# A decoder layer's first feed-forward block: ScalarE and VectorE in written order, five more low halves by adding transfers, one down step moved

## The chip, the cores and the metric

One core of a Trainium2 chip runs the whole layer in one launch. The metric is the device time of a run in microseconds. TensorE (PE) multiplies, VectorE (DVE) and ScalarE (ACT) work elementwise, GpSimd (POOL) and SyncE (SP) here mostly issue transfers.

## The reference

A macaron layer on 512 tokens of width 1024: half a SwiGLU, a mixing stage, half a second SwiGLU, each on an RMS-normed input.

```python
for l in range(DEPTH):
    x = x + 0.5 * swiglu(rms_norm(x, g_ffn1[l]), w_ffn1_gate[l], w_ffn1_up[l], w_ffn1_down[l])
    h = rms_norm(x, g_mix[l])
    proj = h @ w_in[l]
    ...                       # windowed attention, causal conv, attention to 256 memory tokens
    x = x + jnp.concatenate([y_attn, y_conv, y_mem], axis=-1) @ w_out[l]
    x = x + 0.5 * swiglu(rms_norm(x, g_ffn2[l]), w_ffn2_gate[l], w_ffn2_up[l], w_ffn2_down[l])

def swiglu(x, w_gate, w_up, w_down):
    return (jax.nn.silu(x @ w_gate) * (x @ w_up)) @ w_down
```

D_FF is 2816, 22 tiles of 128 hidden channels. All is float32. The change touches the two SwiGLU blocks.

## The kernel before

**Splitting.** x is kept transposed: 8 tiles `x[:, k]` of 128 channels by 512 tokens. Each operand of a product is split into a high half in the short format (float32r) and a low half, the rest: w = hi + lo. A product is three matmuls, hi·hi, hi·lo and lo·hi (`mm3`, L363 to L373, for 512 tokens; `product`, L464 to L471, for 256). The high half is a cast on ScalarE (L173, hidden tiles L427), the low half a subtraction on VectorE (L178, L428). For some weights the low half is made another way ("by queue"): ScalarE writes -hi into the low half's buffer (L175), and POOL issues a transfer that reads the weight from HBM once more and adds it there (L176).

**Weights.** `Weights` holds one list of weight tiles in the order of use. `load_to` issues loads on SP into 4 raw buffers, `split_to` makes hi and lo in 4 split buffers, in list order; `next()` hands out a weight and first splits `conv_ahead` (3) further ones. `load_piece` and `split_piece` do the first two weights by halves.

**A block.** The first tiles are direct (tiles 0 to 3 in block one, 0 to 2 in block two): gate and up are 24 matmuls of 512 tokens each. While they run, VectorE and ScalarE make the blocks of the normed x (`blocks(k)`, k = 0 to 3: seven sums of quarters, split in hi `bh` and lo `bl`) that the remaining, fast tiles need: those are one step of Strassen's scheme (`fast`, 84 matmuls of 256 tokens, weights g, s12, s43, u; the sums s12 and s43 on VectorE, L128 to L131, the second half of u as `vhi` and `vlo`). `evac` multiplies gate and up by the norm's factor `rb` and applies silu; `hidden` splits the result into `hh` and `hl`. xh, xl, hh and hl share a ring of N_ACT = 20 buffers, taken in turn: 16 by xh and xl, then two pairs of hidden tiles; the third hidden tile takes the buffer of xh 0.

**Down steps.** `Plan` divides the hidden tiles into rounds; after a round, the down product of these tiles is added to x, output tile by output tile, each weight load serving two of them. The first round's four loads come in block one as three before tile 4 and one inside tile 5, in block two as four before tile 3. Results of the first two loads go to x by an adding transfer from POOL (L528), the others by VectorE (L531).

**Order.** A scheduler sets every engine's order from its own cost model; nothing is pinned by hand before the change. Ahead of the first tile, the row sums of x² for the norm are gathered on VectorE (L397), reduced on TensorE (L402), turned into factors by a dozen operations on 4 columns (L404 to L407) and spread by four transposes (L415). The first tile's products run over x tiles in the groups `STARTS`.

```python
STARTS = [(0,), (1,), (2, 3), (4, 5), (6, 7)]
PIECES = {(0,): slice(0, 512), (2, 3): slice(512, 1024)}
W.add(down(*d), OTHER if d[0] else WIDE, n == 2 and d[0] == 0)
W.add(flat(gu[f, i]), WIDE, n == 2 and f > 1)
early = self.loads(0) if self.direct < 4 else self.loads(0)[:-1]
```

Of the kernel before, what the change touches and what calls it, by code (L numbers as in the profile page):

```python
# [30 lines left out]
F32 = mybir.dt.float32  # L31
# [4 lines left out]
ALU = mybir.AluOpType  # L36
# [24 lines left out]
PIECES = {(0,): slice(0, 512), (2, 3): slice(512, 1024)}  # L61
# [23 lines left out]
class Weights:  # L85
# [63 lines left out]
    def split_to(self, n):  # L149
        nc = self.nc  # L150
        while self.done < min(n, len(self.items)):
            i = self.done
            need, cols, off, src = self.items[i]
            self.load_to(need + 1)
            if need in self.after:
                self.after.pop(need)()
            if off is None:
                c = (HALF - 128) // 4
                hi, lo = (
                    self.extra.tile([P, cols + 64], F32R, tag=t, name=f"{t}{i}", bufs=1)[:, c : c + cols] for t in ("vhi", "vlo")  # L160
                )
            else:

                j = self.turn % self.bufs[1]
                c = off // 4
                self.turn += 1
                both = self.pool.tile([P, 2048 + 64], F32R, tag=f"w{j}", name=f"w{i}", bufs=1)
                hi, lo = both[:, c : c + 1024], both[:, c + 1024 : c + 2048]
            if i < self.by_hand:
                self.piece[i] = (src(), hi, lo)  # L170
            else:
                raw = src()
                nc.scalar.copy(hi[:, :cols], raw[:, :cols])  # L173
                if i in self.by_queue:
                    nc.scalar.activation(lo[:, :cols], hi[:, :cols].bitcast(F32), AF.Copy, scale=-1.0)  # L175
                    nc.gpsimd.dma_start(self.shaped(lo, self.loads[need]), self.loads[need], accum_op=ALU.add)  # L176
                else:
                    nc.vector.tensor_tensor(lo[:, :cols], raw[:, :cols], hi[:, :cols].bitcast(F32), op=ALU.subtract)  # L178
            self.split[i] = (hi, lo)
            self.done += 1  # L180
            if i >= self.by_hand:
                self.load_to(need + 1 + self.dma_ahead)

    def load_piece(self, i, c):
        self.nc.sync.dma_start(self.piece[i][0][:, c], self.loads[i][:, c])
# [13 lines left out]
class Plan:  # L199
# [12 lines left out]
    def steps(self, f):  # L212
# [4 lines left out]
        if f < second[1]:  # L217
            early = self.loads(0) if self.direct < 4 else self.loads(0)[:-1]
            late = self.loads(0)[len(early) :]
            return early if f == second[0] else [], late if f == second[0] + 1 else [], []  # L220
# [11 lines left out]
def layer(tc, ctx, a):  # L232
# [35 lines left out]
    def ffn_weights(n, memory):  # L268
# [48 lines left out]

    nc.scalar.dma_start(par, a["par"])
    warm = tmp.tile([P, T], BF16, tag="t", name="warm", bufs=5)
# [7 lines left out]
    W.split_to(2)  # L327
# [57 lines left out]
    class Norm:  # L385
# [5 lines left out]
        def add(self, d, engine=POOL):  # L391
            sq = work() if d else tmp.tile([P, T], F32, tag="sqsum", name=nm("sqsum"), bufs=1)
            ACT.activation(sq, x[:, d], AF.Square)
            if d == 0:
                self.sum = sq
            else:
                (engine if d < KT - 1 else DVE).tensor_tensor(self.sum, self.sum, sq, op=ALU.add)  # L397

# [19 lines left out]
    def ffn(pool, norm, first, gain, hooks, next_gain, last):  # L418
# [120 lines left out]

        held = []  # L540
        nxt = Norm()
        raw = {}
        for f in range(NF):
# [714 lines left out]
```

## Time and profile before

| | |
|---|---|
| median of 3 runs | 862.86 us (862.74 to 863.13) |
| the profiled execution | 863.53 us, its span 861.7 us |
| TensorE busy | 851.7 us, 99% of the span, clock granted 0.999 |
| VectorE busy | 692.9 us, 80% |
| ScalarE busy | 453.6 us, 53% |
| POOL busy | 34.0 us, 4% |
| HBM read | 88.07 MB |

A row of a timeline is: start and length in us, engine, line, operation, out<-in, and in brackets how long the engine stood before it and who ended that. Rows of waits are: who waited for whom, us in total, times, the longest. Rows of transfers end with KB each and the us from issue to landing. Line numbers are those of the kernel before.

### The profile page before, as it was taken

To read this page: it belongs to the slowest core of one execution; us is meant where nothing else is said; L and a number is where in the kernel's file an instruction comes from. 1 tells how busy PE (TensorE), PEld (TensorE's weight loads), DVE (VectorE), ACT (ScalarE), POOL (GpSimd) and SP (SyncE) were. 2 spreads that over 40 slices of the span, in tenths; PEclk is the share of its full clock that TensorE was granted. 3 is DMA by queue.
4 is the path that set the end of the run, shared out by engine and by line. 5 is a ranking of instruction groups with operands and counts; after the bars stand their busy time and mean duration, and the time that the engine had idled before them with its cause. 6 is when DMAs were issued, how large, how long until landed. Compare 5 with 4: busy or idle time off the path is not lost.

```text
span 861.7 us, 15812 instructions
## 1 busy us (share of the span) xinstructions
PE 851.7 (99%) x6421; PEld 791.2 (92%) x6421; DVE 692.9 (80%) x1162; ACT 453.6 (53%) x758; POOL 34.0 (4%) x36
## 2 busy tenths in 40 slices
PE   8999999999999999999999999999999999999998
PEld 5889999999999999988676888889999999999998
DVE  6998977787878897869989985899787878687663
ACT  7465555445554444633948764756554545545440
POOL 0000000000000000300000021210000000000000
PEclk9999999999999999999999999999999999999999
DMA  7435333334453434232010323863433343333312
GB/s 269 127 89 149 106 100 121 100 110 136 119 167 119 123 110 129 74 98 62 13 43 21 118 91 102 187 142 110 122 99 123 99 122 98 110 90 121 92 56 99
DMA packets 36217, 94.07 MB, mean 109 GB/s; under 512 B 3376, under 2 KB 7984, under 8 KB 36144
## 3 DMA queue, kind: packets, MB, share of 16 engines
q1 hardware_dynamic: 32032, 85.99, 32.3%
q0 software_dynamic: 2960, 5.51, 3.9%
q10 hardware_dynamic: 1152, 1.57, 0.6%
q8 instruction: 50, 0.82, 0.4%
q14 instruction: 23, 0.19, 0.1%
HBM read 88.07 MB, written 2.10 MB: 105 GB/s over the span
## 4 chain that ended last, share of the span: by engine, by line
PE 91%; DVE 4%; ACT 2%; DMA 1%; issue 1%; SPq 0%; ACTq 0%; DVEq 0%
PE mm L371 15%; PE mm L373 15%; PE mm L372 15%; PE mm L471 11%; PE mm L469 11%; PE mm L470 11%; PE sc L471 2%; PE sc L470 2%; PE sc L469 2%; PE sc L371 1%; PE sc L372 1%; PE sc L373 1%; PE tp L971 1%; DVE w L178 1%; ACT p L936 1%
## 5 line engine op out<-in xcount | busy, mean ns | idle before, releaser
L469 PE MATMUL mm<-bh,w 128*128 128x256 f32 x888 | 245.5, 276 | 0.8 <-ACT kept L484 0.8
L470 PE MATMUL mm<-bl,w 128*128 128x256 f32 x888 | 245.3, 276 | 0.0
L471 PE MATMUL mm<-bh,w 128*128 128x256 f32 x888 | 245.2, 276 | 0.0
L372 PE MATMUL mm<-hl,w 128*128 128x256 f32 (+1 forms) x648 | 185.0, 286 | 0.0
L373 PE MATMUL mm<-hh,w 128*128 128x256 f32 (+1 forms) x648 | 184.9, 286 | 0.0
L371 PE MATMUL mm<-hh,w 128*128 128x256 f32 (+1 forms) x648 | 184.7, 286 | 0.0
L469 PEld LDWEIGHTS mm<-bh,w 128*128 128x128 f32 x888 | 166.7, 188 | 1.1 <-ACT kept L484 1.0
L470 PEld LDWEIGHTS mm<-bl,w 128*128 128x128 f32 x888 | 166.7, 188 | 0.1
L471 PEld LDWEIGHTS mm<-bh,w 128*128 128x128 f32 x888 | 166.7, 188 | 0.0
L173 ACT CAST w<-wraw 128x1024 fp32r<-128x1024 f32 (+2 forms) x123 | 123.3, 1007 | 76.1 <-PE mm L373 23.7
L178 DVE TENSOR_TENSOR w<-wraw,w 128x1024 fp32r<-128x1024 f32 (+2 forms) x117 | 137.0, 1177 | 27.2 <-ACT w L173 23.5
L371 PEld LDWEIGHTS mm<-hh,w 128*128 128x128 f32 x648 | 121.6, 188 | 2.4 <-ACT hh L427 0.3
L373 PEld LDWEIGHTS mm<-hh,w 128*128 128x128 f32 x648 | 121.7, 188 | 2.2
L372 PEld LDWEIGHTS mm<-hl,w 128*128 128x128 f32 x648 | 121.6, 188 | 2.2
L178 DVE TENSOR_TENSOR w<-s,w 128x1024 fp32r<-128x1024 f32 x74 | 90.4, 1222 | 38.1 <-PE mm L471 32.9
L173 ACT CAST w<-s 128x1024 fp32r<-128x1024 f32 x74 | 77.7, 1052 | 23.5 <-PE mm L471 19.1
L371 PE MATMUL mm<-xh,w 128*128 128x512 f32 x176 | 69.7, 400 | 1.9 <-ACT w L189 1.0
L372 PE MATMUL mm<-xl,w 128*128 128x512 f32 x176 | 69.4, 394 | 0.6 <-DVE xl L383 0.5
L373 PE MATMUL mm<-xh,w 128*128 128x512 f32 x176 | 69.1, 393 | 0.0
L531 DVE SCALAR_TENSOR_TENSOR x<-mm,x 128x512 f32<-128x512 f32 x80 | 54.2, 682 | 7.1 <-PE mm L373 7.1
L490 ACT ACTIVATE t<-t 128x512 f32<-128x512 f32 x37 | 23.4, 633 | 68.7 <-DVE t L489 68.7
L128 DVE TENSOR_TENSOR s<-wraw 128x512 f32<-128x512 f32 x37 | 25.6, 691 | 34.5 <-DMA wraw<-in_wgu 34.4
(247 smaller groups left out, 1378.3 us busy)
## 6 DMA issues: line engine op xcount, KB each, us to landing
wraw<-in_wgu SPq DMA_DIRECT2D x86, 512.0 KB, 3.6
wraw<-in_wd SPq DMA_DIRECT2D x38, 512.0 KB, 3.6
wraw<-in_win SPq DMA_DIRECT2D x12, 512.0 KB, 3.5
wraw<-in_wd SPq DMA_DIRECT2D x8, 384.0 KB, 3.3
x<-t POOLq DMA_DIRECT2D x8, 256.0 KB, 4.1
out<-t SPq DMA_DIRECT2D x7, 256.0 KB, 2.0
x<-in_xT SPq DMA_DIRECT2D x3, 512.0 KB, 7.2
wraw<-in_wout_a SPq DMA_DIRECT2D x6, 256.0 KB, 2.7
```

The source lines that it names most:

```text
L128: nc.vector.tensor_tensor(s12[:, l], u[:, l], u[:, r], op=ALU.add)
L173: nc.scalar.copy(hi[:, :cols], raw[:, :cols])
L178: nc.vector.tensor_tensor(lo[:, :cols], raw[:, :cols], hi[:, :cols].bitcast(F32), op=ALU.subtract)
L371: PE.matmul(ps[:, t], wh[:, w], hi(k)[:, t], start=one, stop=False, skip_group_check=cut > 1)
L372: PE.matmul(ps[:, t], wh[:, w], lo(k)[:, t], start=False, stop=False, skip_group_check=cut > 1)
L373: PE.matmul(ps[:, t], wl[:, w], hi(k)[:, t], start=False, stop=end, skip_group_check=cut > 1)
L469: PE.matmul(ps, wh[:, c], bh[k][:, block], start=one, stop=False, skip_group_check=not first)
L470: PE.matmul(ps, wh[:, c], bl[k][:, block], start=False, stop=False, skip_group_check=not first)
L471: PE.matmul(ps, wl[:, c], bh[k][:, block], start=False, stop=end, skip_group_check=not first)
L490: ACT.activation(g, g, AF.Silu)
L531: DVE.scalar_tensor_tensor(o, ps, 0.5, xd, op0=ALU.mult, op1=ALU.add)
L936: ACT.activation(self.p[n, h][:, c], src[h][:, i, c], AF.Exp, scale=self.fac[:, m : m + 1], bias=self.neg[:, m : m + 1], accum_out=self.de ...
```

## The change

Five things. (1) The beginning (transfers of the first pieces, x, the first weights) and ScalarE's and VectorE's work through x's split, the norm's squares and block one's direct tiles is put under `manual_schedule`: these engines then run in the order in which the code stands. TensorE's order is still the scheduler's. (2) The first two weights come in three pieces of 256, 256 and 512 columns, the first from ScalarE's queue, and x tile by tile is multiplied in the order hi, lo, weight's lo, gate and up in turns. (3) In block one the low halves of tile 3's two weights and of the three early down loads are made by queue. (4) `conv_ahead` is 2 in direct tiles of block one, with explicit `ahead(n)` calls; the first `vhi` (item 14) is split by hand at the end. (5) In block two the first round's last down load moves from before tile 3 into tile 4, and its low half is made by VectorE.

```diff
-PIECES = {(0,): slice(0, 512), (2, 3): slice(512, 1024)}
+PIECES = {0: slice(0, 256), 2: slice(256, 512), 4: slice(512, 1024)}
...
-            early = self.loads(0) if self.direct < 4 else self.loads(0)[:-1]
-            late = self.loads(0)[len(early) :]
+            early, late = self.loads(0)[:-1], self.loads(0)[-1:]
...
-                W.add(down(*d), OTHER if d[0] else WIDE, n == 2 and d[0] == 0)
+                W.add(down(*d), OTHER if d[0] else WIDE, True)
...
-                    W.add(flat(gu[f, i]), WIDE, n == 2 and f > 1)
+                    W.add(flat(gu[f, i]), WIDE, f >= 4 - n)
...
+    W.split_to(2)
+    first = tc.manual_schedule(engines={mybir.EngineType.Activation, mybir.EngineType.SP})
+    first.__enter__()
     nc.scalar.dma_start(par, a["par"])
+    for i in range(2):
+        W.load_piece(i, PIECES[0], nc.scalar)
...
-        if ks in PIECES:
+        c = PIECES.get(ks[-1] + 1)
+        if c:
             for i in range(2):
-                W.load_piece(i, PIECES[ks])
+                W.load_piece(i, c, nc.sync)
     W.load_to(4)
-    nc.scalar.dma_start(ident, a["ident"])
+    nc.sync.dma_start(ident, a["ident"])
+    first.__exit__(None, None, None)
...
+        def ahead(n):
+            if not last:
+                W.split_to(n)
...
+        if not last:
+            order.enter_context(tc.manual_schedule(engines={mybir.EngineType.Activation, mybir.EngineType.DVE}))
...
+            W.conv_ahead = 3 if last or f >= plan.direct else 2
...
+                        for k in ks:
+                            w = slice(k * P, (k + 1) * P)
+                            for i, (one, two) in enumerate(((0, xh), (0, xl), (1, xh))):
+                                for ps, both in ((g, (gh, gl)), (u, (uh, ul))):
+                                    PE.matmul(ps, both[one][:, w], two[k], start=k == i == 0, stop=k == 7 and i == 2)
...
                         raw[0] = evac(0, *held)
-                        blocks(0)
                         hidden(0, raw[0])
+                        ahead(6)
                     uh, ul = W.next()
                     mm3(u, uh, ul, range(8), xhk, xlk, True, True)
+                    ahead(7)
                     raw[f] = evac(f, g, u)
                     hidden(f, raw[f])
+                    if f == 1:
+                        ahead(8)
+                        blocks(0)
+                        ahead(9)
+                    if f == 2:
+                        ahead(11)
                     blocks(f)
-                if f == plan.direct - 1 < 3:
-                    blocks(3)
+                if f == plan.direct - 1:
+                    for k in range(f + 1, 4):
+                        blocks(k)
+                    if not last:
+                        W.split_item(14)
+                    order.close()
...
+    with tc.manual_schedule(engines={mybir.EngineType.Activation, mybir.EngineType.DVE}):
+        for k in range(KT):
             scaled_split(k, C_G1)
-        if ks in PIECES:
-            for i in range(2):
-                W.split_piece(i, PIECES[ks])
-    W.split_to(3)
-    for k in range(KT):
-        norm.add(k, DVE)
+            if k in PIECES:
+                for i in range(2):
+                    W.split_piece(i, PIECES[k])
+            if k in (3, 5):
+                sqs[k // 4] = norm.square(k // 4)
+            if k == 6:
+                take(0)
+                take(1)
+        W.split_to(3)
+        for k in range(2, KT):
+            sqs[k] = norm.square(k)
+            if k > 2:
+                take(k - 1)
+        take(KT - 1)
```

The instructions' order at three places. First ScalarE at the start (xh: high half of an x tile, odd numbers 3, 5, 7, 9 for x tiles 0 to 3; w0, w1: the first two weights; sqsum and t: squares). Before:

```order
L382 ACTIVATE xh_3_119<-x_69,par_67 128x512
L393 ACTIVATE sqsum_19_166<-x_69 128x512
L189 CAST w0_93<-wraw0_92 128x512
L189 CAST w1_95<-wraw1_94 128x512
L382 ACTIVATE xh_5_127<-x_69,par_67 128x512
L393 ACTIVATE t_20_168<-x_69 128x512
L382 ACTIVATE xh_7_131<-x_69,par_67 128x512
L393 ACTIVATE t_21_171<-x_69 128x512
L382 ACTIVATE xh_9_135<-x_69,par_67 128x512
```

And of the change (its own line numbers):

```order
L390 ACTIVATE xh_3_126<-x_69,par_67 128x512
L192 CAST w0_75<-wraw0_74 128x256
L192 CAST w1_77<-wraw1_76 128x256
L390 ACTIVATE xh_5_134<-x_69,par_67 128x512
L390 ACTIVATE xh_7_138<-x_69,par_67 128x512
L192 CAST w0_75<-wraw0_74 128x256
L192 CAST w1_77<-wraw1_76 128x256
L390 ACTIVATE xh_9_146<-x_69,par_67 128x512
L401 ACTIVATE sqsum_11_150<-x_69 128x512
L390 ACTIVATE xh_12_152<-x_69,par_67 128x512
```

The squares moved behind x tile 3 and the weights come in quarters, the second quarter behind x tile 2.

Second, ScalarE in block one around hidden tile 2 (hh_58; w9 and w10 the second and third early down load, bh the high half of a block). Before:

```order
L427 CAST hh_48_374<-kept_47_371 128x512
L456 CAST bh_52_382<-braw_50_378 128x768
L173 CAST w9_476<-wraw9_342 128x1024
L460 CAST bh_52_382<-bmade_51_379 128x1024
L436 ACTIVATE t_56_451<-t_56_451 128x512
L173 CAST vhi14_675<-wraw12_479 128x512
L456 CAST bh_62_465<-braw_60_461 128x768
L427 CAST hh_58_457<-kept_57_454 128x512
```

And of the change:

```order
L450 ACTIVATE t_56_468<-t_56_468 128x512
L441 CAST hh_58_474<-kept_57_471 128x512
L177 CAST w9_478<-wraw9_367 128x1024
L179 ACTIVATE w9_478<-w9_478 128x1024
L177 CAST w10_484<-wraw10_383 128x1024
L179 ACTIVATE w10_484<-w10_484 128x1024
L470 CAST bh_62_494<-braw_60_490 128x768
```

Down load w9 was cast ahead of hidden tile 2 and stands behind it now, with its negated copy.

Third, ScalarE in block two around hidden tiles 0 and 1 (w137: the second early down load). Before:

```order
L427 CAST hh_612_6042<-kept_606_6025 128x512
L456 CAST bh_609_6032<-braw_607_6028 128x768
L436 ACTIVATE t_614_6076<-t_614_6076 128x512
L173 CAST w137_6101<-wraw101_5912 128x768
L175 ACTIVATE w137_6101<-w137_6101 128x768
L460 CAST bh_609_6032<-bmade_608_6029 128x1024
L173 CAST vhi143_6325<-wraw105_6135 128x512
L427 CAST hh_616_6082<-kept_615_6079 128x512
```

And of the change:

```order
L441 CAST hh_607_6048<-kept_606_6045 128x512
L177 CAST vhi142_6317<-wraw104_6125 128x512
L470 CAST bh_615_6096<-braw_613_6092 128x768
L177 CAST w137_6121<-wraw101_5932 128x768
L179 ACTIVATE w137_6121<-w137_6121 128x768
L441 CAST hh_611_6088<-kept_610_6085 128x512
L474 CAST bh_615_6096<-bmade_614_6093 128x1024
```

The cast vhi of tile 3's second weight moved ahead of block 0's high half, and reads load 104 instead of load 105.

More of the change, by code (lines that the diff above doesn't have):

```diff
@@ L149, in split_to @@
     def split_to(self, n):
-        nc = self.nc
[L151 to L161, printed above, removed]
-            else:
[L164 to L182, printed above, removed]
@@ L184, in load_piece, with split_item @@
-    def load_piece(self, i, c):
-        self.nc.sync.dma_start(self.piece[i][0][:, c], self.loads[i][:, c])
+        while self.done < min(n, len(self.items)):
+            if self.done not in self.split:
+                self.split_item(self.done)
+            self.done += 1
+    def split_item(self, i):
+        nc = self.nc
+        need, cols, off, src = self.items[i]
+        self.load_to(need + 1)
+        if need in self.after:
+            self.after.pop(need)()
+        if off is None:
+            c = (HALF - 128) // 4
+            hi, lo = (
+                self.extra.tile([P, cols + 64], F32R, tag=t, name=f"{t}{i}", bufs=1)[:, c : c + cols] for t in ("vhi", "vlo")
+            )
+        else:
+            j = self.turn % self.bufs[1]
+            c = off // 4
+            self.turn += 1
+            both = self.pool.tile([P, 2048 + 64], F32R, tag=f"w{j}", name=f"w{i}", bufs=1)
+            hi, lo = both[:, c : c + 1024], both[:, c + 1024 : c + 2048]
+        if i < self.by_hand:
+            self.piece[i] = (src(), hi, lo)
+        else:
+            raw = src()
+            nc.scalar.copy(hi[:, :cols], raw[:, :cols])
+            if i in self.by_queue:
+                nc.scalar.activation(lo[:, :cols], hi[:, :cols].bitcast(F32), AF.Copy, scale=-1.0)
+                nc.gpsimd.dma_start(self.shaped(lo, self.loads[need]), self.loads[need], accum_op=ALU.add)
+            else:
+                nc.vector.tensor_tensor(lo[:, :cols], raw[:, :cols], hi[:, :cols].bitcast(F32), op=ALU.subtract)
+        self.split[i] = (hi, lo)
+        if i >= self.by_hand:
+            self.load_to(need + 1 + self.dma_ahead)
@@ L187, in split_piece, with load_piece @@
+    def load_piece(self, i, c, queue):
+        queue.dma_start(self.piece[i][0][:, c], self.loads[i][:, c])
     def split_piece(self, i, c):
@@ L389, in __init__, with square, take @@
             self.sum = None
-        def add(self, d, engine=POOL):
+        def square(self, d):
             sq = work() if d else tmp.tile([P, T], F32, tag="sqsum", name=nm("sqsum"), bufs=1)
             ACT.activation(sq, x[:, d], AF.Square)
+            return sq
+        def take(self, d, sq, engine):
             if d == 0:
@@ L397, in add @@
                 (engine if d < KT - 1 else DVE).tensor_tensor(self.sum, self.sum, sq, op=ALU.add)
+        def add(self, d, engine=POOL):
+            self.take(d, self.square(d), engine)
         def stats(self):
@@ L542, in ffn @@
         raw = {}
+        order = ExitStack()
+        if not last:
+            order.enter_context(tc.manual_schedule(engines={mybir.EngineType.Activation, mybir.EngineType.DVE}))
         for f in range(NF):
             pre, mid, post = plan.steps(f)
+            W.conv_ahead = 3 if last or f >= plan.direct else 2
             for d in pre:
@@ L555, in ffn @@
                     for ks in first:
-                        mm3(g, gh, gl, ks, xhk, xlk, ks[0] == 0, ks[-1] == 7)
-                        mm3(u, uh, ul, ks, xhk, xlk, ks[0] == 0, ks[-1] == 7)
+                        if len(ks) > 2:
+                            mm3(g, gh, gl, ks, xhk, xlk, ks[0] == 0, ks[-1] == 7)
+                            mm3(u, uh, ul, ks, xhk, xlk, ks[0] == 0, ks[-1] == 7)
+                            continue
+                        for k in ks:
[3 more added lines that the diff above has]
+                                    PE.matmul(ps, both[one][:, w], two[k], start=k == i == 0, stop=k == 7 and i == 2)
                     norm.stats()
@@ L587, in layer, with take @@
     norm = Norm()
-    for ks in STARTS:
-        for k in ks:
-            scaled_split(k, C_G1)
-        if ks in PIECES:
-            for i in range(2):
-                W.split_piece(i, PIECES[ks])
-    W.split_to(3)
-    for k in range(KT):
-        norm.add(k, DVE)
+    sqs = {}
+    def take(k):
+        norm.take(k, sqs.pop(k), DVE)
+    with tc.manual_schedule(engines={mybir.EngineType.Activation, mybir.EngineType.DVE}):
+        for k in range(KT):
+            scaled_split(k, C_G1)
+            if k in PIECES:
[12 more added lines that the diff above has]
+        take(KT - 1)
     mk = keep.tile([P, 2, ML], F32, name="mk")
```

1 line of the change is left out of this document (removed).

## The prediction

> **What bounds the kernel now.** First the page's head, then who TensorE waits for, then stages.
>
> ```profile
> span 861.7 us, 15812 instructions
> PE 851.7 (99%) x6421; PEld 791.2 (92%) x6421; DVE 692.9 (80%) x1162; ACT 453.6 (53%) x758; POOL 34.0 (4%) x36
> ...
> PE tp L326 <- DVE pair L339: 1.2, 1, 1.2
> PE mm L371 <- ACT w L189: 1.0, 1, 1.0
> ...
> PE mm L371 <- ACT xh L382: 0.9, 1, 0.9
> PE mm L469 <- ACT kept L484: 0.8, 1, 0.8
> PE mm L372 <- DVE xl L383: 0.5, 1, 0.5
> ```
>
> TensorE is busy for 851.7 of 861.7 us, and the change removes no matmul from its list. All that any reordering can move is TensorE's waiting: some 10 us in the whole run. The waits that lie where the change works are the start (L326, L371 on the first weight piece and on xh, L372 on xl) and one single wait of 0.8 us in the second block (L469). Everything else that the change does runs beside a busy TensorE and counts only if it makes TensorE wait.
>
> How full the neighbours are in those stages (columns: length; busy time of PE, PEld, DVE, ACT, POOL; granted clock; DMA share; GB/s):
>
> ```profile
> 32.00:64.00 32.00, 32.00 (x142) 26.30 (x141) 31.75 (x47) 17.93 (x23) 1.89 (x2) 1.00 0.25 73
> 535.00:573.00 38.00, 38.00 (x172) 31.40 (x171) 33.47 (x57) 24.72 (x34) 10.07 (x10) 1.00 0.90 188
> ```
>
> In the first block's direct tiles (32 to 64 us) VectorE has no air, 31.75 of 32, while the DMA share is 0.25; in the second block, which already makes low halves by adding transfers, the DMA share is 0.90. The clock is 1.00 throughout. So moving low halves from VectorE to transfers has room in the first block; the question is whether the transfers come in time.
>
> **Part one, the start.** TensorE's rows before:
>
> ```profile
> 6.12 0.50 PE L371 MATMUL mm<-xh,w 128*128 128x512 f32 x1 [1.01 <-ACT w L189]
> 8.86 0.73 PE L371 MATMUL mm<-xh,w 128*128 128x512 f32 x2 [0.91 <-ACT xh L382]
> ...
> 20.71 0.95 PE L402 MATMUL tp<-ones,sqsum 128*128 128x1 f32 x8
> ...
> 32.13 0.39 PE L371 MATMUL sc<-xh,w 128*128 128x512 f32 x1
> ...
> 43.01 0.39 PE L371 MATMUL mm<-xh,w 128*128 128x512 f32 x1
> ```
>
> From 32.13 to 43.01 stand the 48 matmuls of one direct tile, without a wait: 0.227 us each. Tiles 0 and 1 are 96 matmuls, 21.8 us, but they take 32.13 - 6.12 = 26.0 us. About 1.2 of the difference are the norm's row sums (20.71) and transposes; the other 3.0 are waits. They can go in part. What cannot go is the arrival of x:
>
> ```profile
> x<-in_xT SPq DMA_DIRECT2D x1, 512.0 KB, 6.7
> x<-in_xT SPq DMA_DIRECT2D x1, 512.0 KB, 7.9
> ...
> 9.35 0.72 ACT L382 ACTIVATE xh<-x,par 128x512 fp32r<-128x512 f32 x1
> ...
> 10.50 0.71 ACT L382 ACTIVATE xh<-x,par 128x512 fp32r<-128x512 f32 x1
> 11.11 1.13 ACT L189 CAST w<-wraw 128x512 fp32r<-128x512 f32 x2
> 12.14 0.64 ACT L393 ACTIVATE t<-x 128x512 f32<-128x512 f32 x1
> ```
>
> The transfer of x tiles 2 and 3, issued third of the x transfers, took 6.7 us, the last of x 7.9. ScalarE's xh for tile 2 starts at 9.35, so x 2-3 had landed by then. The change puts the same bytes of weights ahead of it (two quarters of each weight now, a half before) and only takes the identity matrix (64 KB) out of the way, so I keep 9.35. From there, in the written order, ScalarE does xh 2 (0.61 to the next start), then the second quarter of the first weight. No 256-wide cast stands in this trace; the pair of 512-wide ones takes 1.13, so 0.57 is the upper end for one and 0.28 the lower, and I take 0.35, an estimate. TensorE's first matmul with tile 2 is then at 9.35 + 0.61 + 0.35 = 10.3, the second weight's at 10.6. Behind it stand 36 matmuls, 8.2 us, and ScalarE keeps ahead of them: six xh at 0.61, two casts at 0.35, two at 0.57, two squares at up to 0.64 are 6.8 us. Tile 0 ends at 10.3 + 8.2 + 0.2 = 18.7. Tile 1 adds 48 matmuls (10.9), the norm's 1.2, and one new wait: the change leaves 11 matmuls (2.5 us) between the row sums and the transposes, and VectorE's chain of twelve small operations between them takes
>
> ```profile
> 21.70 0.16 DVE L404 TENSOR_SCALAR s<-tp 128x4 f32<-128x4 f32 x1 [0.44 <-PE tp L402]
> ...
> 25.96 0.43 DVE L407 COPY t<-rtok 128x512 f32<-128x512 f32 x1
> ```
>
> 4.7 us before, with two low halves of 1.1 each in it that the written order puts elsewhere, so 2.5, and some 0.4 with its hand-overs. Tile 2 starts at 18.7 + 10.9 + 1.2 + 0.4 = 31.2 instead of 32.13: **-1.0**. Ends: if x is never late, the first matmul at 5.5 (the first weight piece is cast ahead of the square, 0.5 us saved) and no wait follows, tile 2 starts 3 us earlier (-2.9); if x 2-3 takes the 7.9 us of the last transfer, the gain is gone (+0.2). I take the row, 6.7.
>
> **Part two, the direct tiles of the first block.** VectorE loses five low halves of about 1.1 us (two of tile 3, three of the early down steps); ScalarE gets five negated copies, POOL five transfers. VectorE's 5.6 us are worth nothing by themselves, since TensorE does not wait there. The new price is a deadline. Hidden tile 2 takes over the buffer of xh 0 (20 buffers: 16 for xh and xl, 4 for two hidden tiles), so ScalarE's copy waits until the third matmul of tile 3's second product has read it. In the written order the cast of down weight 9 and its negation stand behind that copy, and the transfer behind them:
>
> ```profile
> 49.21 0.62 ACT L427 CAST hh<-kept 128x512 fp32r<-128x512 f32 x1
> 49.73 1.04 ACT L173 CAST w<-wraw 128x1024 fp32r<-128x1024 f32 x1
> ...
> 546.50 0.85 ACT L175 ACTIVATE w<-w 128x768 fp32r<-128x768 f32 x1
> ...
> 547.64 1.20 POOL L176 DMA_DIRECT2D w<-in_wd  x1 [4.38 <-ACT w L175]
> ```
>
> After the matmul's 0.39 (the length of all of these) come the copy (0.52 to the next start), the cast (1.05), the negation (1.05 for 1024 columns by the 0.85 for 768), and 0.3 until POOL issues (546.50 + 0.85 = 547.35, issue at 547.64): 3.3 us from that matmul's start. The low half is first read 42 matmuls after it, the rest of the product (21), two down steps of 9 and the third's first two, and the read itself: 9.5 us. The transfer has 9.5 - 3.3 = 6.2 us. What such transfers took in the second block (512 KB twice, then 384 KB):
>
> ```profile
> w<-in_wgu POOLq DMA_DIRECT2D x1, 512.0 KB, 6.4
> w<-in_wgu POOLq DMA_DIRECT2D x1, 512.0 KB, 9.1
> w<-in_wd POOLq DMA_DIRECT2D x1, 384.0 KB, 6.8
> w<-in_wd POOLq DMA_DIRECT2D x1, 384.0 KB, 5.2
> ```
>
> The 9.1 stood behind the 6.4 in one queue. This one stands alone but has 512 KB, in half-size rows, and a weight load of 512 KB beside it. I take 6.8: a wait of **+0.6**. Ends: 0 (at 5.2) and 2.9 (at 9.1). The other four have more time: for tile 3's first weight the cast and negation stand some 8 us ahead of its use. The written order holds nothing else that TensorE needs within those 10 us.
>
> The Trainium skill (DMA: Bandwidth & Descriptors, Anatomy of one DMA, SWDGE path) fits a transfer issued from GpSimd by about 2.0 us plus its bytes over 436 GB/s. For 512 KB that makes an estimate of 3.2 us and no wait here, a sum 0.6 lower. The rows above, 5.2 to 9.1, disagree and decide.
>
> **Part three, the second block.** The removed wait:
>
> ```profile
> 609.04 0.69 DVE L128 TENSOR_TENSOR s<-wraw 128x512 f32<-128x512 f32 x1 [1.87 <-DMA wraw<-in_wgu]
> ...
> 616.24 0.62 ACT L427 CAST hh<-t 128x512 fp32r<-128x512 f32 x1 [1.09 <-DVE t L504]
> ...
> 617.20 0.39 PE L469 MATMUL mm<-bh,w 128*128 128x256 f32 x1 [0.79 <-ACT kept L484]
> ```
>
> Four tiles without a down step (3 to 6) eat the lead of VectorE, whose sums wait for a load at 609; the copy L484 stands on ScalarE behind a hidden tile that is late. With the down step of two times nine wide matmuls (4.1 us) moved into tile 4, VectorE wins as much lead: **-1.0** (0.79, and a slow matmul or two behind it). But the order that the scheduler now makes for ScalarE puts the cast vhi, of tile 3's second weight, right behind hidden tile 0. One down load fewer ahead makes that weight the load of 540.56:
>
> ```profile
> 540.56 0.34 SPq L146 DMA_DIRECT2D wraw<-in_wgu  x1
> wraw<-in_wgu SPq DMA_DIRECT2D x1, 512.0 KB, 6.4
> 543.63 0.62 ACT L427 CAST hh<-kept 128x512 fp32r<-128x512 f32 x1 [1.16 <-DVE kept L439]
> ...
> 559.51 0.62 ACT L427 CAST hh<-kept 128x512 fp32r<-128x512 f32 x1 [0.81 <-DVE kept L439]
> ...
> 560.39 0.39 PE L371 MATMUL mm<-hh,w 128*128 128x512 f32 x1
> ```
>
> It lands at 547.0, beside the adding transfers; ScalarE stands from 544.2 to 547.0. Queued behind it are the high half of block 0, a down cast with its negation, and hidden tile 1. VectorE, which follows ScalarE there, loses about 0.4 at the first, 1.2 at the hidden tile and 0.4 at the next high half, 2.0 us. The third hidden tile was ready at 560.13, its first matmul ran at 560.39: 0.26 to spare. So TensorE waits 2.0 - 0.3 = **+1.7**. Ends: 0 (if the load takes what the loads of the first 80 us take, the row below, or the loss is caught up) and 2.5.
>
> ```profile
> wraw<-in_wgu SPq DMA_DIRECT2D x12, 512.0 KB, 3.6
> ```
>
> Part three: +0.7, between -1.0 and +1.5.
>
> **Sum.** -1.0 + 0.6 + 0.7 = +0.3 on the profiled execution's own 863.53 (its span 861.7 and 1.8 around it), that is 863.8. That execution was 0.67 above the median of the runs, 862.86; on the median's scale 863.2.
>
> **The rivals.** Faster and slower mean over 0.2%, 1.7 us, about what can be told from no change: below 861.1 or above 864.6.
>
> Faster: every transfer is in time. The down weight's transfer takes 6 us or less, the load behind vhi under 5 (VectorE's spare 0.3 and later idle time swallow the rest), and the start keeps its -1.0: -1.0 + 0 - 1.0 = -2.0, 860.9. For it: the 5.2 and the 3.6 of the rows above. Against it: the load at this very place took 6.4. Chance 0.29.
>
> Slower: the adding transfers become the bound. The place is the first matmul of the third early down step in block one, the price what the transfer needs beyond 6.2 us. At the 9.1 us of the row above it is 2.9: -1.0 + 2.9 + 0.7 = +2.6, 865.5. It decides from 8.2 us on. For it: ScalarE releases raw buffers at both casts, so two weight loads run in just this stretch; against it: nothing else stands in POOL's queue. Chance 0.23.
>
> The start is paced by x anyway and the written order brings nothing there: 0 + 0.6 + 0.7 = +1.3, 864.2, still no change. Chance 0.12. The forecast itself, 863.2 with its own range 861.8 to 864.6, has 0.36. Together: faster 0.29, same 0.48, slower 0.23. The range takes most of both sides: 860.2 (start 0.7 better than in the faster case) to 865.6.
>
> **What would show it.** Start: tile 2's first matmul (32.13 before) at 31.2; at 29.5 the x transfer was not the pace, at 32 the order brought nothing. Middle: a TensorE wait at L373's place in the third early down step on a transfer into w, 0.6 long; none means that the transfer took under 6.2. Second block: ScalarE idle before vhi for 2 to 3 us on a DMA, a TensorE wait on hh of 1.7 some 4 us into the down steps, and no wait on L484's copy in tile 6. The prediction is wrong if TensorE waits in places that I have not named, in the transition to the fast tiles above all, or if neither of the two new waits shows.

## The result: 0.9 per cent slower

The changed kernel took 870.92 us (median of 6 runs, 870.08 to 873.97), the kernel before 863.05 beside it (862.74 to 865.15 in 6 runs). The ratio is 1.009, 95% interval 1.0075 to 1.0105: 7.9 us slower. Forecast were 863.2, and at the outside 865.6.

The profiled execution took 871.11 us. The head of its page and, from the view of TensorE's waits, who it waited for (total, times, longest, us):

```profile
span 869.3 us, 15828 instructions
...
PE 856.6 (99%) x6421; PEld 793.7 (91%) x6421; DVE 691.7 (80%) x1160; ACT 458.8 (53%) x764; POOL 38.1 (4%) x40
```

```profile
PE mm L381 <- DMA w<-in_wd: 2.3, 1, 2.3
PE mm L379 <- ACT hh L441: 2.3, 1, 2.3
PE tp L333 <- DVE pair L347: 1.2, 1, 1.2
...
PE mm L379 <- DVE t L449: 0.8, 1, 0.8
PE mm L483 <- ACT kept L498: 0.4, 1, 0.4
PE mm L586 <- ACT w L192: 0.4, 1, 0.4
```

The start's waits have shrunk (0.4 on a weight piece is left of 2.4), and the 0.8 on L484's copy in block two is gone. In their place stand a wait of 2.3 on an adding transfer, one of 2.3 on a hidden tile and one of 0.8 on VectorE. Less what has gone, these waits are well short of the loss. The span grew by 7.6, and TensorE's busy time by 4.9, with the same 6421 matmuls. Busy time that grows without more work points to slower matmuls.

**Where it went.** Both traces hold the same matmuls in nearly the same order, so matmul n of the one can be set against matmul n of the other. The shift between them (after minus before) changes at few places:

| place | shift behind it | change | what stands there |
|---|---|---|---|
| start, tiles 0 and 1 | -1.3 | -1.3 | waits gone |
| third early down step, block one, first matmul | -0.4 | +1.0 | bank not yet read by VectorE |
| its third matmul | +2.2 | +2.5 | low half of down weight 9 |
| the matmuls behind it | +3.8 | +1.6 | half clock |
| early down steps, block two | +6.2 | +2.4 | hidden tile 2 |
| the matmuls behind it | +7.8 | +1.6 | half clock |
| tiles 3 to 21 of block two, end | +7.7 | -0.1 | the fifth fast tile better, the third worse |

The start and the middle, row by row (start, length, engine, line, tiles; in brackets the idle time before it and what ended it):

```profile
5.86 0.79 PE L586 MATMUL mm<-xh,w 128*128 128x512 f32 x1
7.03 0.50 PE L586 MATMUL mm<-xh,w 128*128 128x512 f32 x1 [0.37 <-ACT w L192]
...
8.02 0.72 ACT L390 ACTIVATE xh<-x,par 128x512 fp32r<-128x512 f32 x1 [0.42 <-DMA x<-in_xT]
...
30.90 0.39 PE L379 MATMUL sc<-xh,w 128*128 128x512 f32 x1
...
47.19 0.69 DVE L449 TENSOR_TENSOR t<-sc,rb 128x512 f32<-128x512 f32 x1
...
49.36 0.62 ACT L441 CAST hh<-kept 128x512 fp32r<-128x512 f32 x1 [0.81 <-DVE kept L453]
...
52.31 1.20 POOL L180 DMA_DIRECT2D w<-in_wd  x1 [8.07 <-ACT w L179]
...
54.80 0.96 DVE L475 TENSOR_TENSOR bl<-braw,bh 128x768 fp32r<-128x768 f32 x1 [1.13 <-ACT bh L470]
...
56.90 0.69 DVE L449 TENSOR_TENSOR t<-mm,rb 128x512 f32<-128x512 f32 x1
57.73 0.47 PE L379 MATMUL mm<-hh,w 128*128 128x512 f32 x1 [0.83 <-DVE t L449]
...
60.75 0.47 PE L381 MATMUL mm<-hh,w 128*128 128x512 f32 x1 [2.32 <-DMA w<-in_wd]
```

Its transfer, from the view of issues (KB, us from issue to landing):

```profile
w<-in_wd POOLq DMA_DIRECT2D x1, 512.0 KB, 8.3
```

Tile 2 starts at 30.90, 1.2 earlier than before. The adding transfer of down weight 9 is issued at 52.31 and lands 8.3 us later, at 60.6; TensorE would have read it at 57.2, half a microsecond into a step that could have begun at 56.75. And the step's first matmul had waited already: its bank was that of tile 3's gate product, and VectorE read it only at 56.90, after the blocks. What follows the wait, in windows of one microsecond (busy time and number of PE, PEld, DVE, ACT, POOL, then granted clock, DMA share, GB/s):

```profile
60.00:61.00 1.00, 0.25 (x1) 0.28 (x2) 0.40 (x1) 0.56 (x1) 0.00 (x0) 1.00 1.11 203
61.00:62.00 1.00, 1.00 (x5) 0.78 (x5) 1.00 (x3) 0.00 (x0) 0.00 (x0) 0.78 1.07 197
62.00:63.00 1.00, 1.00 (x4) 0.81 (x3) 0.97 (x2) 0.00 (x0) 0.00 (x0) 0.50 0.21 35
...
64.00:65.00 1.00, 1.00 (x4) 0.77 (x3) 0.26 (x1) 0.00 (x0) 0.00 (x0) 0.51 0.00 0
65.00:66.00 1.00, 1.00 (x6) 0.82 (x5) 0.00 (x0) 0.00 (x0) 0.00 (x0) 1.00 0.00 0
```

The clock stays full through the standstill, falls to 0.50 almost a microsecond after TensorE has gone on, and comes back some 3.4 us later (0.4 us of it in the second window, 1.0 in each of the next three). Such a stretch is not the profiled execution's alone: the mean granted clock of the six runs is 0.993 to 0.996, against 0.998 to 1.000 in 54 runs of the kernel before, and one stretch of 3.4 us at half clock takes 0.002 of it. Block two, the same way, with the load that vhi waits for:

```profile
544.30 0.34 SPq L146 DMA_DIRECT2D wraw<-in_wgu  x1
...
551.24 0.62 ACT L177 CAST vhi<-wraw 128x512 fp32r<-128x512 f32 x1 [3.31 <-DMA wraw<-in_wgu]
...
554.11 0.60 ACT L441 CAST hh<-kept 128x512 fp32r<-128x512 f32 x1
...
565.89 0.62 ACT L441 CAST hh<-kept 128x512 fp32r<-128x512 f32 x1 [1.47 <-DVE kept L453]
...
566.56 1.94 PE L379 MATMUL mm<-hh,w 128*128 128x512 f32 x4 [2.30 <-ACT hh L441]
```

```profile
wraw<-in_wgu SPq DMA_DIRECT2D x1, 512.0 KB, 6.9
```

ScalarE stands 3.31 us ahead of the cast vhi, hidden tiles 1 and 2 come late, and TensorE waits 2.30 after 18 matmuls, 4.1 us, of the down steps. The four matmuls behind it take 1.94, twice their usual time.

### The profile page after: what moved, and what is told of

Its sections match the earlier page's. It is cut to its first block, busy times and chain, and to the rows that moved or that the text cites. A ratio compares the mean times of both kernels' runs of the same rounds, so it can differ in the third digit from the quotient of the medians.

```text
span 869.3 us, 15828 instructions
## 1 busy us (share of the span) xinstructions
PE 856.6 (99%) x6421; PEld 793.7 (91%) x6421; DVE 691.7 (80%) x1160; ACT 458.8 (53%) x764; POOL 38.1 (4%) x40
## 4 chain that ended last, share of the span: by engine, by line
PE 85%; DVE 5%; issue 4%; ACT 3%; DMA 2%; POOL 0%; ACTq 0%; POOLq 0%; DVEq 0%
PE mm L379 12%; PE mm L381 12%; PE mm L380 12%; PE mm L483 12%; PE mm L484 12%; PE mm L485 12%; PE sc L483 2%; PE sc L484 2%; PE sc L485 2%; PE mm L586 1%; DMA wraw<-in_wgu 1%; PE tp L1024 1%; DMA w<-in_wd 1%; ACT p L989 1%; PE tp L1038 1%
## 5 line engine op out<-in xcount | busy, mean ns | idle before, releaser
L484 PE MATMUL mm<-bl,w 128*128 128x256 f32 x888 | 245.2, 276 | 0.0
L381 PE MATMUL mm<-hh,w 128*128 128x256 f32 (+1 forms) x648 | 185.9, 287 | 2.3 <-DMA w<-in_wd 2.3
L484 PEld LDWEIGHTS mm<-bl,w 128*128 128x128 f32 x888 | 166.7, 188 | 0.1
L182 DVE TENSOR_TENSOR w<-wraw,w 128x1024 fp32r<-128x1024 f32 (+2 forms) x113 | 132.0, 1174 | 28.5 <-ACT w L177 24.7
L381 PEld LDWEIGHTS mm<-hh,w 128*128 128x128 f32 x648 | 122.2, 189 | 5.2 <-ACT hh L441 2.7
L379 PE MATMUL mm<-xh,w 128*128 128x512 f32 x158 | 63.0, 399 | 0.0
L380 PE MATMUL mm<-xl,w 128*128 128x512 f32 x158 | 62.1, 393 | 0.1
L381 PE MATMUL mm<-xh,w 128*128 128x512 f32 x158 | 62.0, 392 | 0.0
```

The lines of the kernel that those rows point to most:

```text
L379: PE.matmul(ps[:, t], wh[:, w], hi(k)[:, t], start=one, stop=False, skip_group_check=cut > 1)
L380: PE.matmul(ps[:, t], wh[:, w], lo(k)[:, t], start=False, stop=False, skip_group_check=cut > 1)
L381: PE.matmul(ps[:, t], wl[:, w], hi(k)[:, t], start=False, stop=end, skip_group_check=cut > 1)
L484: PE.matmul(ps, wh[:, c], bl[k][:, block], start=False, stop=False, skip_group_check=not first)
```

## The experiments

Two lengths make them comparable. Block one's is from the first matmul of tile 2 to the first of the fast tiles: 38.3 us before, 43.4 after. Block two's is from the first matmul of the down steps to the first of the fast tiles. With three early loads it holds one load (4.1) less, and 16.40 before would be 12.3; after has 16.43.

| kernel | median, us | ratio to before (95%) | block one | block two |
|---|---|---|---|---|
| changed kernel | 870.92 | 1.0090 (1.0075 to 1.0105) | 43.4 | 16.4, for 12.3 |
| e1, step put back | 868.78 | 1.0057 (1.0041 to 1.0074) | 44.8 | 16.3, for 16.4 |
| e2, weight 9 earlier | 864.70 | 1.0022 (1.0009 to 1.0036) | 39.0 | 14.1, for 12.3 |
| e3, filled wait | 868.04 | 1.0049 (1.0030 to 1.0069) | 41.7 | 13.7, for 12.3 |
| e4, no adding transfers | 876.66 | 1.0144 (1.0119 to 1.0169) | 47.9 | 18.0, for 12.3 |
| e5, vhi behind hidden 2 | 867.77 | 1.0050 (1.0036 to 1.0064) | 41.8 | 12.3 |
| e6, start alone | 862.93 | 0.9992 (0.9983 to 1.0001) | 38.6 | 16.6, for 16.4 |
| e7, e2 and e1 | 863.01 | 0.9995 (0.9986 to 1.0005) | 39.0 | 16.3, for 16.4 |
| e8, e2 and e5 | 863.61 | 1.0000 (0.9991 to 1.0009) | 39.0 | 12.3 |
| e10, start and step | 862.34 | 0.9983 (0.9974 to 0.9992) | 38.5 | 12.3 |

### e1: the down step put back

```diff
-            early, late = self.loads(0)[:-1], self.loads(0)[-1:]
+            early = self.loads(0) if self.direct < 4 else self.loads(0)[:-1]
+            late = self.loads(0)[len(early) :]
```

> The changed kernel with the second block's fourth early down load put back ahead of tile 3 (its plan as before). Theory A: the moved load alone makes ScalarE's cast vhi stand for 3.3 us on a transfer, and the 2.3 us wait on hidden tile 2 with the slow-clock stretch behind it follow from that. Then both go (-2.4 and -1.6), the old wait of 0.8 in tile 6 comes back in place of 0.5 in tile 4: 871 - 3.7 = about 867.3. Rival B: the wait in block two comes from elsewhere (block one's lateness, the adding transfers of that block); then a wait of more than 1 us stays at the same place and the time is 869.5 or more.

The wait on hh is gone and block two is as long as before; the old wait on L484's copy (L499 here) is back. It stands 384 matmuls behind the first fast one, and a fast tile has 84, so it is in the fifth fast tile, number 7, and not 6 as the prediction has it. Lines are one higher in this kernel:

```profile
PE mm L382 <- DMA w<-in_wd: 2.8, 1, 2.8
...
PE mm L484 <- ACT kept L499: 0.9, 1, 0.9
```

Theory A holds in the trace: from ahead of block two's wait to behind it, this execution gains 4.2 us on the changed kernel. The median fell only 2.1, not 3.7, and the profiled execution shows why. Its down weight 9 landed later still, TensorE waited 2.8 us, and the low clock lasted 6.8 us, until 67.1, so block one lost 1.4 more.

### e2: weights 8 and 9 split earlier in block one

```diff
-                    ahead(7)
+                    ahead(10 if f == 2 else 7)
```

> The changed kernel with down weights 8 and 9 cast, negated and sent ahead of tile 2's evacuation in block one (some 3 us earlier) instead of behind hidden tile 2. Theory A: the transfer of 8.3 us was issued too late; now it is issued at about 48.5 and lands at about 57, the wait of 2.3 on it is gone or under 0.4, the slow clock behind it too, and the bank wait of 0.8 goes because block 2's casts on ScalarE come 2 us earlier: -1.0 - 2.5 - 1.6 = -5.1, about 865.8. Rival B: the transfers are the bound in this stretch (DMA share 0.99) and an earlier issue only makes them slower or makes the third one late: a wait of over 1.5 us on a transfer stays, the time is above 869.

```profile
48.21 1.20 POOL L180 DMA_DIRECT2D w<-in_wd  x1 [4.11 <-PE mm L381]
...
57.36 0.50 PE L379 MATMUL mm<-hh,w 128*128 128x512 f32 x1 [0.59 <-DVE t L449]
57.70 0.39 PE L380 MATMUL mm<-hl,w 128*128 128x512 f32 x1
57.93 0.40 PE L381 MATMUL mm<-hh,w 128*128 128x512 f32 x1
```

Issued 4.1 us earlier, the transfer takes 7.1 and lands at 55.3; L381 runs without a wait and the clock stays full. Block one loses 0.8 us against before instead of 5.1: theory A. So the transfer was not the bound; it was asked for too late (and it took 1.2 us less at the earlier place). The bank wait did not go, it shrank from 0.83 to 0.59: that part of theory A was wrong. Block two's wait was shorter here than in the changed kernel (1.5, and a full clock behind it), which is why the gain is 6.2 and not 5.1. Two of the ten runs were at 868.7, with a mean clock of 0.995 and 0.998 where the six runs at 864 have 1.000; they were not traced.

### e3: the wait filled with work

```diff
+                if r == 0 and not last and d == 2:
+                    spare = tp_bank()
+                    for i in range(13):
+                        PE.matmul(spare, wh[:, :P], h_hi[0], start=i == 0, stop=i == 12)
```

> The changed kernel with 13 extra 128x512 matmuls into an unused bank ahead of the third early down step of block one, so that TensorE works through the wait there (2.95 us of work that nobody reads). Theory A: the half clock for 3 us is the consequence of TensorE standing still for 2.3 us; without the standstill the clock stays at 1.00 there, and only there (the second block's stretch keeps 0.50): more matmuls, yet 1.3 to 1.6 us less, about 869.5. Rival B: the clock is lowered by something else at that time (transfers, the power of the chip): 0.50 shows at 62 to 65 us as before, and the time is 871 or a little more.

```profile
56.71 3.11 PE L535 MATMUL tp<-hh,w 128*128 128x512 f32 x13
59.65 0.39 PE L379 MATMUL mm<-hh,w 128*128 128x512 f32 x1
...
61.13 0.40 PE L381 MATMUL mm<-hh,w 128*128 128x512 f32 x1
```

```profile
62.00:63.00 1.00, 1.00 (x6) 0.80 (x5) 0.97 (x2) 0.94 (x2) 0.05 (x1) 1.00 0.13 23
63.00:64.00 1.00, 1.00 (x6) 0.81 (x5) 0.93 (x3) 0.87 (x2) 1.00 (x2) 1.00 0.00 0
```

The matmul that needs weight 9 runs 0.4 us later than in the changed kernel, and still block one is 1.7 us shorter, with 13 matmuls (2.9 us) more in it: the clock is 1.00 at 62 to 64. That fits theory A, but the control failed it: block two's wait was only 1.1 here (ScalarE had to wait 2.12 for vhi's load, not 3.31) and showed no low clock either. The profiled execution is the fastest of four: it gains 4.6 us on the changed kernel's, 2.8 of them in block two, where the median of the runs gains 2.9 in all.

### e4: block one's low halves back on VectorE

```diff
-                W.add(down(*d), OTHER if d[0] else WIDE, True)
+                W.add(down(*d), OTHER if d[0] else WIDE, n == 2 and d[0] == 0)
...
-                    W.add(flat(gu[f, i]), WIDE, f >= 4 - n)
+                    W.add(flat(gu[f, i]), WIDE, n == 2 and f > 1)
```

> The changed kernel with the five low halves of block one back on VectorE (no adding transfers there), the written order kept. Theory A: the adding transfers are at fault in block one, and VectorE still has the air for the low halves: the waits there vanish, about 866. Rival B: the written order leaves VectorE and ScalarE waiting for each other in turns and has no room for 5.7 us more of VectorE's work (it stood idle for some 4.7 of the 31 us): tile 3's first copy comes some 4 us later, TensorE waits 3 to 4 us for a bank at the third early down step, and the clock drops there too: 870 to 873.

```profile
PE mm L379 <- DVE t L449: 6.8, 1, 6.8
```

```profile
54.54 2.36 DVE L182 TENSOR_TENSOR w<-wraw,w 128x1024 fp32r<-128x1024 f32 x2 [0.26 <-ACT w L177]
...
63.14 0.68 DVE L449 TENSOR_TENSOR t<-mm,rb 128x512 f32<-128x512 f32 x1
```

Rival B, and harder than it had said: the bank of tile 3 is read at 63.14 instead of 56.90. The five low halves, of 1.1 to 1.2 us, stand in the written order ahead of it. Block one is 4.5 us longer than in the changed kernel. Block two's wait was 3.9 here, and the profiled execution, the slowest of four, has one more stretch at half clock in the mixing stage (464.5). So the adding transfers are what keeps this written order from costing still more; the order itself is the tight part.

### e5: the cast vhi behind hidden tile 2

```diff
-            ACT.copy(h_hi[f], t)
+            cast = ACT.copy(h_hi[f], t)
...
+            if last and f == 2:
+                W.anchor, W.issue_after = cast.ins, tc.issue_after
...
-            nc.scalar.copy(hi[:, :cols], raw[:, :cols])
+            behind = self.issue_after(self.anchor) if off is None and self.anchor is not None else ExitStack()
+            with behind:
+                nc.scalar.copy(hi[:, :cols], raw[:, :cols])
```

> The changed kernel, all parts kept, with one instruction of block two moved: ScalarE's cast vhi, which stood 3.3 us on its load ahead of hidden tile 1, is queued behind hidden tile 2. Theory A: the place of this cast on ScalarE makes hidden tile 2 late, not the moved down step itself; the wait of 2.3 us on hh and the slow clock behind it go (-2.4 - 1.6), about 866.9; block one stays as it was. Rival B: hidden tile 2 is late because VectorE or the adding transfers are; then a wait of over 1 us stays there and the time is above 869.

Lines are some five to seven higher in this kernel:

```profile
562.59 0.63 ACT L446 CAST hh<-kept 128x512 fp32r<-128x512 f32 x1 [1.33 <-DVE kept L460]
564.07 0.61 ACT L180 CAST vhi<-wraw 128x512 fp32r<-128x512 f32 x1
```

Theory A: with one instruction moved, hidden tile 2 is cast 3.3 us earlier (2.8 when counted from the start of the down steps), vhi finds its load landed, TensorE has no wait in block two's down steps, and their length is the 12.3 of an undisturbed one. The moved down step does no harm; where the scheduler then put vhi did. The same trace held a surprise in block one, where nothing had been changed:

```profile
60.78 0.47 PE L386 MATMUL mm<-hh,w 128*128 128x512 f32 x1 [2.36 <-DMA w<-in_wd]
```

```profile
62.00:63.00 1.00, 1.00 (x6) 0.83 (x5) 0.97 (x2) 0.00 (x0) 0.00 (x0) 1.00 0.13 21
```

As long a wait as in the changed kernel, and a full clock behind it. So e3 alone had proved nothing about the clock, and a run that varies only the standstill was needed.

### e9: standstills on purpose

In the kernel before, 29 of the 37 fast tiles (the expectation's 31 is a miscount) got this ahead of their first product, with n of 2, 4, 7, 10, 14, 18 or 23 fills of 16 columns (one execution, of 955 us; only its standstills are used):

```diff
+                PE.matmul(ps[:, :16], w0[0][:, :P], probe, start=True, stop=True)
+                for _ in range(n):
+                    POOL.memset(probe.bitcast(F32), 0.0)
+                PE.matmul(ps[:, :16], w0[0][:, :P], probe, start=True, stop=True)
```

> The kernel before with standstills of TensorE put in on purpose: ahead of 31 of the 37 fast tiles, a matmul that reads a small tile, 2, 4, 7, 10, 14, 18 or 23 small fills of that tile by GpSimd, and a second matmul that reads it again (their results are not used); TensorE's order in those tiles is the written one. Waits of some 0.5 to 5 us each, in steady stretches with a full clock. Theory A: the wait's length alone decides: none of the waits up to 1.7 us is followed by a clock of 0.50, every one over 2.8 us is, by 3 us or more of it, and those between go either way. Rival B: the clock falls for another reason that was near in the two blocks (transfers at full share): then long waits here are followed by a full clock, or short ones by a low one.

Two equal standstills:

```profile
263.44 0.28 PE L487 MATMUL tp<-probe,w 128*128 128x16 f32 x1 [1.83 <-POOL probe L486]
...
664.76 0.28 PE L487 MATMUL tp<-probe,w 128*128 128x16 f32 x1 [1.83 <-POOL probe L486]
```

and two microseconds from one microsecond behind each:

```profile
264.40:266.40 2.00, 2.00 (x11) 2.00 (x11) 0.37 (x1) 0.08 (x1) 0.00 (x0) 0.50 0.26 49
665.80:667.80 2.00, 2.00 (x20) 2.00 (x19) 1.08 (x2) 0.37 (x1) 0.00 (x0) 1.00 0.83 242
```

Eleven matmuls in 2 us against twenty. Counted over all of them:

| standstill of TensorE, us | followed by half clock |
|---|---|
| 0.42 to 0.48 | 0 of 5 |
| 0.82 | 0 of 4 |
| 1.33 | 0 of 4 |
| 1.83 | 2 of 4 |
| 2.51 | 2 of 3 |
| 3.16 to 3.19 | 4 of 4 |
| 4.03 | 4 of 4 |

(The 29th stood right behind a matmul that had waited 2.64 for a transfer, waited for nothing itself, and was followed by half clock too.) Theory A: the standstill does it, without any transfer of the two blocks near it; in 665.80 to 667.80 the DMA share is 0.83 and the clock full. Its limits held as far as they were tried (nothing between 1.33 and 1.83 was), but the length alone does not decide: the same 1.83 goes both ways. A slow stretch cost 16 slow matmuls of 256 columns in nearly every case, 0.213 us each instead of 0.113, that is 1.6 us, whether the standstill was 1.83 or 4.03.

**Where a standstill falls.** Most of what the table leaves to chance can be read from the same trace. The 13 slow stretches behind standstills begin 6, 6, 6, 24, 6, 9, 7, 101, 6, 6, 35 and 6 times 3.413 us apart; twelve last 3.41 us and one 6.83. So in this execution the clock changed on a fixed grid of steps of 3.41 us. The two equal standstills lie differently on it: the first is whole in one step, the second is cut into 0.24 and 1.60. Here are the two steps (length, busy time of PE, the rest of the row as above; length less busy time is the idle time):

```profile
260.39:263.80 3.41, 1.58 (x15) 1.48 (x14) 3.41 (x7) 2.52 (x5) 1.97 (x11) 1.00 0.94 261
663.16:666.57 3.41, 1.81 (x15) 1.81 (x16) 3.38 (x5) 1.50 (x2) 1.03 (x10) 1.00 0.43 126
```

Counted by the idle time in one step at full clock, up to 1.72 us was never followed by half clock, 1.83 in two cases of three, and 1.86 or more in all eleven. The 2.51 that stayed free was cut into 1.72 and 0.78. The other traces agree. The changed kernel's two waits of 2.3 each lie whole in one step (the first below); e5's 0.83 and 2.36 are cut into steps with 1.64 and 1.54 idle (second and third row), and e2's 1.5 is short of the limit. A step already at half clock with 1.15 to 2.26 us idle was followed by another one (e9, e1, e4): hence the 6.8 us of e1.

```profile
58.15:61.57 3.42, 1.10 (x6) 0.72 (x5) 2.74 (x5) 0.72 (x2) 0.00 (x0) 1.00 1.13 208
...
55.82:59.23 3.41, 1.78 (x7) 0.86 (x5) 3.41 (x5) 1.48 (x2) 0.00 (x0) 1.00 1.05 235
59.23:62.64 3.41, 1.86 (x8) 1.60 (x9) 2.70 (x5) 0.62 (x1) 0.00 (x0) 1.00 0.94 171
```

The grid lies elsewhere in every trace, counted from the start of the span, so which wait is hit stays a matter of chance. Three slow stretches, all at one place of the mixing stage (e4, e5 and e10), follow no standstill. In these traces one step ahead of them holds a whole group of 16 matmuls of two columns (1.84 us); in the nine others the grid cuts that group, at most 1.69 us lie in one step, and no slow stretch follows. That such narrow matmuls count like idle time is a guess from this; no run varied them.

### e6, e7, e8 and e10: the parts put together again

e6 is the kernel before with the start's part alone. e7 is e2 and e1 in one, e8 is e2 and e5 in one. e10 is e6 with the later down step and vhi queued as in e5; block one's direct tiles are those before. Their edits are the ones shown.

> The kernel before with the start's part alone: the weights in three pieces, the written order of ScalarE and VectorE through the scaling and the norm, the k in turns in tile 0, and nothing of the two blocks. Theory A: the start is worth the 1.2 us that the first matmul of tile 2 shows (30.90 against 32.13) and nothing gives it back: 863.3 - 1.2 = about 862.1. Rival B: VectorE, with 31.75 of 32 us busy in block one, is the pace there, so a TensorE that starts earlier waits later and the end stays within 0.4 of 863.3.

> Both repairs so far together: down weights 8 and 9 earlier in block one, and block two's fourth down load back ahead of tile 3. Theory A (the causes add): 864.7 less 2.1 for the hh wait, less 0.5 for the wait in tile 4, plus 0.9 for the one in tile 6: about 863.0, no change against before, since the start's 1.2 is offset by the bank wait of 0.6 and scatter. Rival B (something else of the change still costs): over 864.5.

> Down weights 8 and 9 earlier in block one, the later down step of block two kept, and its vhi cast queued behind hidden tile 2. Theory A: only the start's gain, the bank wait of 0.6 and the small wait in tile 4 are left: 864.7 less 2.1 = about 862.4, faster than before by 0.1 per cent. Rival B: the cast vhi, now late, makes the first fast tile wait for its weight: over 863.5.

> The start's part and the later down step of block two (its vhi cast queued behind hidden tile 2), without the change's block one. Theory A: both keep what their places showed: the start 0.7 (measured alone), tile 6's wait of 0.8 gone or halved: 863.2 - 0.7 - 0.6 = about 862.0. Rival B: a new wait in the first fast tiles or in tile 4 takes the second part back: 862.8 or more, as with the start alone.

**e6** lies between its two theories. Tile 2 starts at 31.07, 1.1 earlier; block one gives 0.1 back (its 38.6 also holds two matmuls of the first fast tile, which TensorE took earlier here); the median is 0.7 lower, and the interval reaches 1.0001. **e7** came out as theory A said, 863.01 for 863.0: the two causes add, and nothing else of the change costs more than the interval of 0.9 us either way can hide. **e8** missed its 862.4: with both waits gone the time is that of before. Rival B's wait in the first fast tile did not come. In its profiled execution tile 2 started only at 32.19, held up by a weight piece in tile 0, and one wait was new:

```profile
PE mm L490 <- ACT kept L505: 0.6, 1, 0.6
```

This is the copy that was late in the fifth fast tile before (L484 there), now in the third, one tile behind the moved down step; the changed kernel has it with 0.4, e10 with 0.6. The moved step mostly moved that wait. **e10** is the version that beats both kernels, by 0.17 per cent against before (0.08 to 0.26), about what theory A gave and just under what I had called a difference; it is the change without its middle part, and with vhi placed by hand.

## Why the prediction was wrong

| term | forecast | measured | |
|---|---|---|---|
| start | -1.0 | -1.3 | near, but partly by luck |
| bank of the third early down step | none | +1.0 | left out |
| down weight 9 | +0.6 | +2.5 | issue 1.3 later, transfer 1.5 longer |
| half clock behind it | none | +1.6 | not seen |
| hidden tile 2 in block two | +1.7 | +2.4 | mechanism right |
| half clock behind it | none | +1.6 | not seen |
| L484's wait and the rest | -1.0 | -0.1 | wait moved to the third fast tile |
| sum | +0.3 | +7.7 | |

**The places were right.** Both waits that the prediction named as tests showed, at the line, on the instruction and after the number of matmuls that it gave: the third early down step on the transfer into w, and hh some 4 us into block two's down steps, behind ScalarE standing 3.31 (2 to 3 had been said) ahead of vhi. The start came out at 30.90 for 31.2, but partly by luck: the prediction has the arrival of x as its pace, at 9.35, and x's tiles 2 and 3 had landed by 8.02. TensorE's last wait in tile 0 was the 0.37 us on a weight piece, ended at 7.03; behind it no wait shows in tile 0. The bank wait of 0.83 is a place that the prediction did not name, one of its own signs of being wrong. The rival that stood for "slower" was this transfer too, with a price of 2.9 at most.

**The step of part two that failed** is its deadline of 6.2 us. The chain from hidden tile 2's copy to POOL's issue was right (2.95 for 2.9). But the copy was to start when the third matmul of tile 3's second product had read the buffer, here at 47.68 + 0.39 = 48.1; it started at 49.36, on VectorE's `kept`. In the written order blocks 0 and 1 stand ahead of tile 2's evacuation, and VectorE took tile 2's bank at 47.19. So the start's gain never reached this chain: the copy was at 49.21 before. That left 4.9 us. The transfer took 8.3, not 6.8, with a DMA share above 1.0 beside it. Landed at 60.6 against 57.2, it was 3.4 late: the 0.6 of the forecast, 1.3 and 1.5. Part of these 3.4 shows as the bank wait of 1.0, which stands ahead of it in the same step. The sentence that failed with it is "the written order holds nothing else that TensorE needs within those 10 us": it held tile 3's first copy, behind a block whose low halves wait for ScalarE (54.80). e2 shows what that wait costs by itself, and e4 what it would have cost without the transfers.

**What was missing altogether** is the clock. The prediction read 1.00 throughout before and let a wait cost its length: "all that any reordering can move is TensorE's waiting" is the second step that failed, with 3.2 of the 7.4 us that the forecast missed. Before, no wait behind the start was longer than 1.0 us, and the standstills of e9 up to 1.33 lower nothing; at 2.3 it depends on where the grid lies, and the changed kernel lost 1.6 us at both places. The Trainium skill (TensorE: Matmul & The Clock Gate, HAM oscillation) warns of gaps above about 3.4 us. By that rule 2.3 us would have been harmless; the runs disagree, 1.83 was enough in 2 of 4. The Trainium skill, on the same page (Part 1), has a free-running window of about 3.4 us decide. The traces agree with that: the slow stretches keep to a grid of 3.41 us, and equal waits end differently.

**Part three** had the right instruction; the load took 6.9 for 6.4, and the loss reached TensorE as 2.4 for 1.7. Its gain of 1.0 was wrong: the wait on L484's copy went from the fifth fast tile to the third. Why it is the third was not tried.

The prediction also weighed the Trainium skill's fit for transfers issued by GpSimd (DMA: Bandwidth & Descriptors, Anatomy of one DMA), 3.2 us for 512 KB by estimate. The five in block one took 6.3 to 8.8.

**Open** are why weight 9's transfer took 8.3 to 8.8 at that place and 7.1 four microseconds earlier (two weight loads ran beside it, but no run took them away), and why the start scatters: TensorE's waits on weight pieces in tile 0 add up to 0.4 us in the changed kernel and to 1.4 in e8.

## What to carry to other kernels

Price a new wait of TensorE by its length up to about 1.3 us, and from 1.8 us on add a slow stretch behind it (here 1.6 us), with a chance. With a limit of 1.8 us idle in a step of 3.41 and the grid anywhere, an estimate from e9's numbers is one half for a wait of 1.8 us, two thirds for 2.5 and certainty from 3.6 on. Two small waits are cheaper than a long one only if they do not lie within one step. Where an order is written out, a transfer's deadline counts from when its issuing engine really gets there: follow each engine's queue through the whole stage, since time won ahead of a queue does not arrive behind it when the queue holds other work first (VectorE's blocks here). And look at what a moved load does to the instructions that a scheduler places: the cast that did the damage in block two was not part of the change.

## What the runs showed of the hardware that was not expected

The granted clock falls to 0.50 after standstills of TensorE as short as 1.83 us, in 2 of 4 cases, never in 13 up to 1.33, and in all 8 from 3.16 on. What counts is the idle time in one step of a 3.41 us grid: none up to 1.72 us, two of three at 1.83, all eleven from 1.86 on in e9. In the changed kernel the fall came almost 1 us after work had gone on (full at 60 to 61 us, 0.50 from 62), so a trace shows it behind the wait, on matmuls that wait for nothing. Filling a wait with matmuls that nobody reads made the kernel faster in e3, though e5 shows that a wait of the same length is free when the grid cuts it.
